# A hybrid decoder trunk on one core: x's scales inside the transposing matmul, convolution buffers of their own, and the weights' low parts split over two engines

## The chip, the cores and the metric

The kernel runs on one core of one Trainium2 chip. The metric is the device time of one execution in microseconds. Three runs of the kernel before are given, with a median of 2076.28 us, and one of its executions was profiled.

A core has a matrix engine (TensorE, PE in the profile; its weight loads are PEld), a vector engine (VectorE, DVE), an activation engine (ScalarE, ACT), a general engine (GpSimd, POOL) and a queue that issues most transfers (SyncE, SP). Each engine works through its own list of instructions in order and waits where an operand is not ready.

## The reference

One decoder layer over 2048 tokens of 1024 channels. The normalised input goes through one projection, whose columns feed three groups of heads; their gated outputs are joined, projected back and added to the input.

```python
u = rms_norm(h, norm_g[l])
proj = jnp.einsum('bsd,de->bse', u, w_in[l])
(q, k, v, z_att, f_raw, z_ssd, xbc, dt_raw, x_lru, z_lru) = jnp.split(proj, split_points, axis=-1)
log_f = jax.nn.log_sigmoid(f_raw + forget_b[l])
y_att = fox_attention(q, k, v, log_f, q_norm_g[l], k_norm_g[l]) * jax.nn.silu(z_att)
y_ssd = ssd_mixer(xbc, dt_raw, z_ssd, ...)      # causal convolution, silu, chunked scan, gated norm
y_lru = rglru_mixer(x_lru, ...) * jax.nn.silu(z_lru)   # causal convolution, gates, associative scan
mix = jnp.concatenate([y_att, y_ssd, y_lru], axis=-1)
h = h + jnp.einsum('bse,ed->bsd', mix, w_out[l])
```

`rms_norm` divides each token's row by the root of its mean square and multiplies by a gain for each channel. Everything is float32.

## The kernel before, in words

PE multiplies in a rounded float32 (`F32R`). A float32 operand is split into a high part (rounded by a cast) and a low part (the remainder, by a subtraction), and each product is made of three matmuls: high times high, and the two mixed ones. So u exists as `uh`, `ul` and a weight tile as `wh`, `wl`.

The stages, in the order in which PE meets them (times of the profiled execution):

- **x** (9 to 67 us). x is loaded in 16 tiles `xt` of 128 tokens by 1024 channels, four tiles to a block of tokens `tb`. For each tile ACT squares and sums (L255, with an accumulator read), DVE and ACT make `rs` = 1/root (L127 to L131), DVE scales the tile by it (L264, in block 0), and PE transposes it in 128x128 pieces (L279, the float32 identity as one operand) into a PSUM tile `pu`, one for each of 8 slices k of 128 channels. ACT writes `uh` from `pu` (L282) and DVE `ul` (L283).
- **Convolution groups** (16 to 322 us). Six groups of 256 columns (`pxx`, `proj_ch`, L331 to L333), each 4 token blocks by 2 halves, 24 matmuls of 128x512 a piece. Each piece goes through `conv`: ACT copies it out of PSUM into `rtx` (L376), ACT starts the sum `accx` (L381), DVE adds three more taps (L384), ACT takes tanh (L409, into a buffer `thx`), DVE multiplies; the result goes to DRAM, by PE transposes for the first groups and straight from `accx` for the last (`ct_d`). Group 0 runs between the transposes of x.
- **pvz** (322 to 376 us): 280 columns for all 16 token tiles (`proj_tok`, L305 to L307). DVE reads its last columns for `dt` (L367).
- **LRU** (377 to 596 us), four groups m of 128+128 columns: projections `pll` and `pzl`, each convolution and split again into `xhl`, `xll`, gates `pga`, `pgx` (L561 to L563), then on DVE reciprocals (L569), a scan over 1024 tokens (L585) and on POOL and ACT the gate path.
- **zs** (582 to 774 us): four groups of 256 columns, two token tiles into one PSUM tile (`proj_tok2`, L318 to L320). Then the same function for q, k and v, z of attention, with units of the SSD scan between them (to 1275 us).
- **Attention and output projection**, to the end.

What sets the order: the kernel text states the work, and a scheduler with a cost simulation (`schedule_with_timeline_sim=True`) fixes each engine's list when the kernel is built. A change of buffers or of the engine of one instruction can so move others.

Weights: `weights()` (L178) loads 8 tiles of 128 rows for each group into raw buffers `wr` (pool `wrp`, 4 buffers), casts each on ACT (L192) and subtracts on the engine `eng` (L193): DVE by default, POOL for the LRU groups and the first two zs groups. The pool `wp` holds `NSL` = 9 tiles `wh` and as many `wl`, one more than a group has.

Buffers: the convolution's pool `cvp` (tags `acc`, `thx`, `stx`, 2 buffers each) is opened after the pools of the x stage are closed, and `accx` has two buffers.

Of the kernel before, what the change touches and what calls it, by code (L numbers as in the profile page):

```python
# [18 lines left out]
P = 128  # L19
# [7 lines left out]
NEG = -1.0e30  # L27
NSL = 9
NQ = 4
# [18 lines left out]
def hybrid_block(ctx, tc, x, norm_g, w_in, q_norm_g, k_norm_g, forget_b, ssd_conv_w, ssd_conv_b,  # L48
# [128 lines left out]

    def weights(cols, rawp=wrp, eng=V):  # L178

        n = sum(w for _, w in cols)  # L180
        i = gcount[0]
        gcount[0] += 1
        wh, wl = [], []
        for k in range(KD):
            raw = rawp.tile([P, n], F32, name=f"wr{i}_{k}", tag="wr")
            h = wp.tile([P, n], F32R, name=f"wh{i}_{k}", tag="wh")
            l = wp.tile([P, n], F32R, name=f"wl{i}_{k}", tag="wl")
            o = 0
# [3 lines left out]
            A.copy(h, raw)  # L192
            eng.tensor_tensor(l, raw, h.bitcast(F32), op=ALU.subtract)  # L193
            wh.append(h)
            wl.append(l)
        return wh, wl, n

    rtx = ExitStack()
    rtp = rtx.enter_context(tpool(name="rtp", bufs=2, side="right"))
    with tpool(name="p0", bufs=2) as p0, tpool(name="p01", bufs=1) as p01, \  # L200
            tpool(name="px", bufs=XB) as px:
# [43 lines left out]
        def c1(name, i=0):  # L245
            j = CV[name] + i
            return cv[:, j:j + 1]

        def norm_x(tb):
            ss = p0.tile([P, 4], F32, name=f"ss{tb}", tag="ss")  # L250
            rs = p0.tile([P, 4], F32, name=f"rs{tb}", tag="rs")
            for i in range(4):
                t = tb * 4 + i
                sq = p01.tile([P, D], BF16, name=f"sq{t}", tag="sq")
                A.activation(sq, xts[t], AF.Square, accum_out=ss[:, i:i + 1])  # L255
                if tb == 0:
                    rsqrt1(p0, rs[:, i:i + 1], ss[:, i:i + 1], 1.0 / D, f"r0{t}")
            if tb > 0:
                V.tensor_scalar(ss, ss, 1.0 / D, EPS, op0=ALU.mult, op1=ALU.add)
                rsqrt(p0, rs, ss, 4, f"r0{tb}")  # L260
            for i in range(4):
                xt = xts[tb * 4 + i]
                if tb == 0:
                    V.tensor_scalar(xt, xt, rs[:, i:i + 1], -1.0, op0=ALU.mult, op1=ALU.mult)  # L264
                elif i < NDV:
# [6 lines left out]
        for tb in range(4):  # L272
            if tb + AHEAD < 4:
                norm_x(tb + AHEAD)
            for k in range(KD):
                pt, tag = ((psY, "Y"), (pst, "pt"))[(tb * KD + k) % 5 % 2]
                pt = pt.tile([P, 512], F32, name=f"pu{tb}_{k}", tag=tag)
                for i in range(4):
                    T.transpose(pt[:, i * P:(i + 1) * P],  # L279
                                xts[tb * 4 + i][:, k * P:(k + 1) * P], ident)  # L280
                g = ngc[:, k:k + 1]
# [27 lines left out]

    def proj_tok2(w, t2, name, space=None):  # L310
        wh, wl, n = w
        pp, tag = space or (psj, "pj")
        ps = pp.tile([P, 2, 256], F32, name=name, tag=tag)
        for i in range(2):
            t = t2 * 2 + i
            h, l, sl = uh[t // 4], ul[t // 4], slice(t % 4 * P, t % 4 * P + P)
            for k in range(KD):
                T.matmul(ps[:, i, :], h[k][:, sl], wh[k], start=(k == 0), stop=False)  # L318
                T.matmul(ps[:, i, :], h[k][:, sl], wl[k], start=False, stop=False)  # L319
                ins = T.matmul(ps[:, i, :], l[k][:, sl], wh[k], start=False, stop=(k == KD - 1))  # L320
        anchor[0] = ins
# [51 lines left out]

    def conv(pool, ps, prev, wname, bname, m, nm, ntile, acc, tag="", rtp=None):
        rt = (rtp or pool).tile([P, 515], F32, name=f"rt{nm}", tag="rt" + tag)
        A.copy(rt[:, 3:515], ps)  # L376
# [12 lines left out]
    g0 = g0x.enter_context(tpool(name="g0", bufs=2))  # L389
    with tpool(name="cvp", bufs=2) as pool, tpool(name="cl", bufs=1) as cl:  # L390
        for gq in range(6):
# [9 lines left out]
            for tb in range(4):  # L401
                for mm in range(2):
                    m = gq * 2 + mm
                    nm = f"x{m}_{tb}"
                    ps = proj_ch(w, mm, tb, f"px{nm}")
                    acc = pool.tile([P, 512], F32, name=f"acc{nm}", tag="acc")
                    prev[mm] = conv(pool, ps, prev[mm], "cw", "cb", m, nm, 12, acc, str(mm), rtp)
                    th = pool.tile([P, 512], F32, name=f"thx{nm}", tag="thx")
                    A.activation(th, acc, AF.Tanh)  # L409
# [4 lines left out]
                    if m < 10:  # L414
                        pt = pst.tile([P, 4, P], F32, name=f"ptx{nm}", tag="pt")
                        for i in range(4):
                            T.transpose(pt[:, i, :], acc[:, i * P:(i + 1) * P], ident)
                        st = pool.tile([P, 4, P], F32, name=f"st{nm}", tag="stx")
                        A.copy(st, pt)
# [670 lines left out]
```

## Time and profile before

| quantity | value |
|---|---|
| runs | 2074.33, 2076.28, 2081.79 us (median 2076.28) |
| profiled execution | 2074.41 us, its span 2072.7 us |
| PE busy | 2002.1 us, 97% of the span |
| PEld busy | 1759.0 us, 85% |
| DVE busy | 1246.1 us, 60% |
| ACT busy | 975.9 us, 47% |
| POOL busy | 568.9 us, 27% |
| bytes moved | 265.18 MB, mean 128 GB/s |

The time of an execution and its span differ by 1.7 us, which lie outside the profile. In rows of the timeline the columns are the start, the busy time, engine, line, operation, output and inputs, tile shape, count, and in brackets the idle time before and what ended it. In windows each engine has its busy time and its number of instructions, and `PEclk` is the granted clock of PE as a share of full speed. Durations of matmuls overlap, so that the time that one costs in a stream is the distance between two starts.

### The profile page before, as it was taken

Reading aid. Unit: us, or ns where it says so; the run is one execution under the profiler, and the core shown is the slowest. Engines: PE = TensorE matmul, PEld = TensorE weight load, DVE = VectorE, ACT = ScalarE, POOL = GpSimd, SP = SyncE. Lnnn points to the kernel's source line nnn. Section 1 sums busy time; section 2 is a strip of 40 time slices with the busy share of each in tenths; the row PEclk is TensorE's granted clock in tenths of the full one; section 3 lists DMA queues with packets and bytes.
Section 4 is the critical chain, followed back from the end, with each engine's and each line's share of the span. In section 5 each row is a group of like instructions: output and inputs, shape, how many; then the busy total and the mean of one; then the engine's idle time right before and its main releaser. Section 6 shows DMA issues by size and latency. Waiting matters only on the chain. (4 is left out here: it accounts for less than half of the span.)

```text
span 2072.7 us, 36031 instructions
## 1 busy us (share of the span) xinstructions
PE 2002.1 (97%) x12485; PEld 1759.0 (85%) x12485; DVE 1246.1 (60%) x2656; ACT 975.9 (47%) x2053; POOL 568.9 (27%) x814
## 2 busy tenths in 40 slices
PE   7999999999999999999998999999998999999999
PEld 6788888887789998887887998888887888888887
DVE  6655455388875226776566345667767777775333
ACT  7444443366652124554444234566666666664110
POOL 0000001355531004454553001243332333323110
PEclk9999999999999999999999999999999999999999
DMA  5122233111123225666655726575475375443443
GB/s 197 41 70 63 62 113 102 44 42 43 42 62 99 69 76 148 197 196 191 195 173 161 214 85 218 159 200 160 131 192 163 115 193 151 133 129 91 136 142 117
DMA packets 287317, 265.18 MB, mean 128 GB/s; under 512 B 59780, under 2 KB 227232, under 8 KB 285088
## 3 DMA queue, kind: packets, MB, share of 16 engines
q1 hardware_dynamic: 286976, 262.85, 43.3%
q8 instruction: 99, 1.62, 0.3%
q14 instruction: 82, 0.67, 0.1%
q0 software_dynamic: 160, 0.03, 0.1%
HBM read 168.22 MB, written 94.57 MB: 127 GB/s over the span
## 5 line engine op out<-in xcount | busy, mean ns | idle before, releaser
L918 DVE TENSOR_TENSOR pl<-T,ph 128x512 fp32r<-128x512 f32 (+2 forms) x352 | 191.1, 565 | 70.8 <-ACT ph L917 69.5
L980 PE MATMUL po<-woh,mh 128*128 128x512 f32 x512 | 213.0, 416 | 8.9 <-DVE xr L988 4.7
L917 ACT CAST ph<-T 128x512 fp32r<-128x512 f32 (+2 forms) x352 | 161.9, 490 | 122.6 <-PE T L910 84.9
L981 PE MATMUL po<-wol,mh 128*128 128x512 f32 x512 | 201.5, 394 | 0.0
L982 PE MATMUL po<-woh,ml 128*128 128x512 f32 x512 | 200.5, 397 | 0.0
L910 PE MATMUL T<-ident,L 128*128 128x128 f32 x1088 | 172.6, 276 | 2.4 <-ACT L L860 1.5
L860 ACT ACTIVATE L<-L,mx 128x1920 f32<-128x1920 f32 (+15 forms) x128 | 154.5, 1208 | 39.7 <-DVE mx L857 35.2
L384 DVE SCALAR_TENSOR_TENSOR accx<-rtx,cv,accx 128x512 f32<-128x512 f32 x144 | 104.5, 752 | 90.9 <-ACT accx L381 76.0
L331 PE MATMUL pxx<-uh,wh 128*128 128x512 f32 x384 | 153.0, 401 | 4.8 <-ACT rtx L376 3.3
L319 PE MATMUL pqk<-wl,uh 128*128 128x256 f32 x512 | 153.6, 301 | 2.6 <-DVE wl L193 2.6
L896 PE MATMUL O<-ph,vv 128*128 128x256 f32 x576 | 153.8, 288 | 2.0 <-ACT ph L917 1.9
L332 PE MATMUL pxx<-ul,wh 128*128 128x512 f32 x384 | 153.9, 402 | 0.0
L897 PE MATMUL O<-pl,vv 128*128 128x256 f32 x576 | 152.2, 289 | 1.0 <-DVE pl L918 0.7
L333 PE MATMUL pxx<-uh,wl 128*128 128x512 f32 x384 | 152.8, 399 | 0.0
L318 PE MATMUL pqk<-wh,uh 128*128 128x256 f32 x512 | 147.1, 292 | 3.1 <-ACT wh L192 3.1
L320 PE MATMUL pqk<-wh,ul 128*128 128x256 f32 x512 | 149.5, 294 | 0.0
L319 PE MATMUL pzs<-wl,uh 128*128 128x256 f32 x512 | 144.8, 284 | 3.2 <-POOL wl L193 3.1
L320 PE MATMUL pzs<-wh,ul 128*128 128x256 f32 x512 | 144.5, 283 | 0.0
L318 PE MATMUL pzs<-wh,uh 128*128 128x256 f32 x512 | 143.2, 283 | 0.0
L648 ACT ACTIVATE ab<-ab,nacs 128x128 f32<-128x128 f32 x256 | 82.6, 391 | 125.9 <-POOL ab L644 125.7
L849 POOL TENSOR_SCALAR_AFFINE_SELECT cm<-cb 128x384 f32<-128x384 f32 (+3 forms) x128 | 58.9, 463 | 297.8 <-DVE mx L857 145.3
L910 PEld LDWEIGHTS T<-ident,L 128*128 128x128 f32 x1088 | 127.4, 141 | 13.5 <-ACT L L860 5.4
(315 smaller groups left out, 5600.9 us busy)
## 6 DMA issues: line engine op xcount, KB each, us to landing
ab<-acs_d SPq DMA_DIRECT2D x64, 256.0 KB
pt_d<-xr SPq DMA_DIRECT2D x64, 256.0 KB
wr<-in_w_in_dram SPq DMA_DIRECT2D x192, 64.0 KB
wr<-in_w_in_dram SPq DMA_DIRECT2D x80, 128.0 KB
xt<-in_x_dram SPq DMA_DIRECT2D x16, 512.0 KB
xs_d<-stx SPq DMA_DIRECT2D x32, 256.0 KB
v_d<-vs SPq DMA_DIRECT2D x32, 256.0 KB
zs_d<-zs SPq DMA_DIRECT2D x32, 256.0 KB
```

The lines of the kernel that those rows point to most:

```text
L318: T.matmul(ps[:, i, :], h[k][:, sl], wh[k], start=(k == 0), stop=False)
L319: T.matmul(ps[:, i, :], h[k][:, sl], wl[k], start=False, stop=False)
L320: ins = T.matmul(ps[:, i, :], l[k][:, sl], wh[k], start=False, stop=(k == KD - 1))
L332: T.matmul(ps, wh[k][:, ms], ul[tb][k], start=False, stop=False)
L860: A.activation(lt[:, 0:n], lt[:, 0:n], AF.Exp, bias=mx, scale=-1.0, accum_out=sm[:, i:i + 1])
L896: T.matmul(po[:, ca], vv[:, kt, :], ph[:, jj, ca], start=(kt == 0), stop=False)
L910: ins = T.transpose(pt[:, jj, i * P:(i + 1) * P], L[i][:, kt * P:(kt + 1) * P], ident)
L917: A.copy(ph[:, ja, ca], pt[:, ja, ca])
L918: V.tensor_tensor(pl[:, ja, ca], pt[:, ja, ca], ph[:, ja, ca].bitcast(F32), op=ALU.subtract)
L980: T.matmul(ps, mh[:, j, :], h, start=(j == 0), stop=False)
L981: T.matmul(ps, mh[:, j, :], l, start=False, stop=False)
L982: T.matmul(ps, ml[:, j, :], h, start=False, stop=(j == 3))
```

## The change

1. **x, block 0.** The tiles are no longer scaled (L264 falls away). Instead DVE writes `dg`, the identity times `-rs`, 128x128 for each of the four tiles, and PE multiplies the 128x128 piece of x with `dg` in an ordinary float32 matmul in place of the transpose (32 of them). Tiles 1 and 3 are squared on DVE, 0 and 2 on ACT as before. The table for the square root is loaded ahead of all of it.
2. **Convolution buffers.** `cvp` (now for `stx` and `dg`) and `cv3` (`acc`, 3 buffers) are opened ahead of the pools of x and share no memory with them. The tanh goes into the first 512 columns of the `rtx` tile, so that there is no `thx`.
3. **`NSL`** is 8 and no longer 9.
4. **`proj_tok2`** runs k outside and the two token tiles inside: a weight tile serves six matmuls in a row.
5. **Low parts.** In the LRU groups and the first two zs groups, POOL subtracts for even k and DVE for odd k.

The diff, cut to its core:

```diff
-NSL = 9
+NSL = 8
-    def weights(cols, rawp=wrp, eng=V):
+    def weights(cols, rawp=wrp, eng=(V,)):
-            eng.tensor_tensor(l, raw, h.bitcast(F32), op=ALU.subtract)
+            eng[k % len(eng)].tensor_tensor(l, raw, h.bitcast(F32), op=ALU.subtract)
...
+    cvp = rtx.enter_context(tpool(name="cvp", bufs=2, side="right"))
+    cv3 = rtx.enter_context(tpool(name="cv3", bufs=3, side="right"))
...
+        dg = cvp.tile([P, 4, P], F32, name="dg", tag="stx")
+        A.activation(p01.tile([P, 1], F32, name="tab"), eps, AF.Sqrt)
...
+                if tb == 0 and i % 2:
+                    sq = cv3.tile([P, D], BF16, name=f"sq{t}", tag="acc")
+                    V.tensor_tensor_reduce(sq, xts[t], xts[t], 1.0, 0.0, ALU.mult, ALU.add,
+                                           ss[:, i:i + 1])
+                else:
...
                 if tb == 0:
                     rsqrt1(p0, rs[:, i:i + 1], ss[:, i:i + 1], 1.0 / D, f"r0{t}")
+                    V.tensor_scalar(dg[:, i, :], ident, rs[:, i:i + 1], -1.0, op0=ALU.mult,
+                                    op1=ALU.mult)
...
-                    V.tensor_scalar(xt, xt, rs[:, i:i + 1], -1.0, op0=ALU.mult, op1=ALU.mult)
+                    continue
...
-                    T.transpose(pt[:, i * P:(i + 1) * P],
-                                xts[tb * 4 + i][:, k * P:(k + 1) * P], ident)
+                    xk = xts[tb * 4 + i][:, k * P:(k + 1) * P]
+                    if tb == 0:
+                        T.matmul(pt[:, i * P:(i + 1) * P], xk, dg[:, i, :], start=True, stop=True)
+                    else:
+                        T.transpose(pt[:, i * P:(i + 1) * P], xk, ident)
...
-        for i in range(2):
-            t = t2 * 2 + i
-            h, l, sl = uh[t // 4], ul[t // 4], slice(t % 4 * P, t % 4 * P + P)
-            for k in range(KD):
-                T.matmul(ps[:, i, :], h[k][:, sl], wh[k], start=(k == 0), stop=False)
+        for k in range(KD):
+            for i in range(2):
+                t = t2 * 2 + i
+                h, l, sl = uh[t // 4], ul[t // 4], slice(t % 4 * P, t % 4 * P + P)
+                last = k == KD - 1
+                T.matmul(ps[:, i, :], h[k][:, sl], wh[k], start=(k == 0 and i == 0), stop=False,
+                         skip_group_check=True)
...
-    with tpool(name="cvp", bufs=2) as pool, tpool(name="cl", bufs=1) as cl:
+    with tpool(name="cl", bufs=1) as cl:
...
-                    acc = pool.tile([P, 512], F32, name=f"acc{nm}", tag="acc")
-                    th = pool.tile([P, 512], F32, name=f"thx{nm}", tag="thx")
+                    acc = cv3.tile([P, 512], F32, name=f"acc{nm}", tag="acc")
+                    th = prev[mm][:, 0:512]
...
-            w = weights([(C_XL + m * P, P), (C_ZL + m * P, P)], eng=G)
+            w = weights([(C_XL + m * P, P), (C_ZL + m * P, P)], eng=(G, V))
...
-            w = weights([(C_ZS + gq * 256, 256)], eng=G if gq < 2 else V)
+            w = weights([(C_ZS + gq * 256, 256)], eng=(G, V) if gq < 2 else (V,))
```

How it moves instructions, at the three places of which the prediction speaks. In the lists, the first number of a name is the token block or tile, or the slice k of a weight tile, and the last is a running number that differs between the two kernels.

At the head, DVE's list of the kernel before, from the low parts of the first weight tiles to the scaling of the fourth tile of x:

```order
L193 TENSOR_TENSOR wl_0_235<-wr_0_233,wh_0_234 128x256
L193 TENSOR_TENSOR wl_1_241<-wr_1_239,wh_1_240 128x256
L129 RECIPROCAL rs_323<-r_t 128x1
L193 TENSOR_TENSOR wl_2_247<-wr_2_245,wh_2_246 128x256
L130 SCALAR_TENSOR_TENSOR r_t<-rs_323,r_h 128x1
L193 TENSOR_TENSOR wl_3_253<-wr_3_251,wh_3_252 128x256
L131 SCALAR_TENSOR_TENSOR rs_323<-r_t,rs_323 128x1
L264 TENSOR_SCALAR xt_231<-xt_231,rs_323 128x1024
```

The same place of the changed kernel, from the second low part to the fourth tile's `dg`; the square of the fourth tile, an operation named ISA, stands four rows further up, with the first low part behind it:

```order
L193 TENSOR_TENSOR wl_1_247<-wr_1_245,wh_1_246 128x256
L219 COPY ngc<-pr 128x8
L128 TENSOR_SCALAR r_h<-ss_331 128x1
L130 SCALAR_TENSOR_TENSOR r_t<-rs_332,r_h 128x1
L193 TENSOR_TENSOR wl_2_253<-wr_2_251,wh_2_252 128x256
L129 RECIPROCAL rs_332<-r_t 128x1
L193 TENSOR_TENSOR wl_3_259<-wr_3_257,wh_3_258 128x256
L131 SCALAR_TENSOR_TENSOR rs_332<-r_t,rs_332 128x1
L130 SCALAR_TENSOR_TENSOR r_t<-rs_332,r_h 128x1
L268 TENSOR_SCALAR dg<-ident,rs_332 128x128
L131 SCALAR_TENSOR_TENSOR rs_332<-r_t,rs_332 128x1
L268 TENSOR_SCALAR dg<-ident,rs_332 128x128
```

The third tile's `dg` and the fourth's have moved behind the square on DVE and behind all four low parts; before, the third tile was scaled ahead of the low parts and only the fourth behind them.

At the end of the convolution groups, ACT's list of the kernel before, from a copy of the last block to the last tanh (pvz's own copies L356 and L362 stand between):

```order
L409 ACTIVATE thxx_2_2951<-accx_2_2943 128x512
L356 ACTIVATE vs_0_3110<-pvz_0_3112 128x2x64
L356 ACTIVATE vs_0_3110<-pvz_1_3137 128x2x64
L356 ACTIVATE vs_1_3178<-pvz_2_3180 128x2x64
L381 ACTIVATE accx_3_2980<-rtx_3_2981,cv 128x512
L362 ACTIVATE th_0_0_3164<-pvz_0_3112 128x128
L362 ACTIVATE th_0_1_3171<-pvz_1_3137 128x128
L381 ACTIVATE accx_3_3017<-rtx_3_3018,cv 128x512
L362 ACTIVATE th_1_0_3232<-pvz_2_3180 128x128
L409 ACTIVATE thxx_3_2988<-accx_3_2980 128x512
L409 ACTIVATE thxx_3_3025<-accx_3_3017 128x512
```

The same place of the changed kernel:

```order
L397 COPY rtx_3_2941<-pxx_3_2915 128x512
L192 CAST wh_0_2998<-wr_0_2997 128x280
L402 ACTIVATE accx_3_2940<-rtx_3_2941,cv 128x512
L192 CAST wh_1_3007<-wr_1_3006 128x280
L192 CAST wh_2_3016<-wr_2_3015 128x280
L192 CAST wh_3_3025<-wr_3_3024 128x280
L192 CAST wh_4_3034<-wr_4_3033 128x280
L431 ACTIVATE rtx_3_2941<-accx_3_2940 128x512
L397 COPY rtx_3_2977<-pxx_3_2951 128x512
L192 CAST wh_5_3043<-wr_5_3042 128x280
L402 ACTIVATE accx_3_2976<-rtx_3_2977,cv 128x512
L192 CAST wh_6_3052<-wr_6_3051 128x280
```

Before, the last four sums L381 and tanhs stand behind the weight casts and behind copies of pvz's own results; now each piece is copied, summed and put through tanh within a few rows, with the casts of pvz's weights between.

At the boundary between two LRU groups, DVE's list of the kernel before, around the first scan of a group, beside which the next group's weights are made:

```order
L584 TENSOR_TENSOR XC_0_4606<-XC_0_4606,MM_0_4711 128x1024
L585 SCALAR_TENSOR_TENSOR MM_0_4711<-RA_0_4710,XC_0_4606 128x1024
L588 COPY hc_0_4821<-MM_0_4711 128x1
L589 SCALAR_TENSOR_TENSOR ZZ_0_4679<-MM_0_4711,ZZ_0_4679 128x1024
L568 TENSOR_SCALAR RA_1_4922<-RA_1_4922 128x512
L569 RECIPROCAL RA_1_4922<-RA_1_4922 128x512
L568 TENSOR_SCALAR RA_1_4922<-RA_1_4922 128x512
```

The same place of the changed kernel:

```order
L607 SCALAR_TENSOR_TENSOR MM_0_4670<-RA_0_4669,XC_0_4565 128x1024
L193 TENSOR_TENSOR wl_1_4937<-wr_1_4935,wh_1_4936 128x256
L610 COPY hc_0_4780<-MM_0_4670 128x1
L611 SCALAR_TENSOR_TENSOR ZZ_0_4638<-MM_0_4670,ZZ_0_4638 128x1024
L193 TENSOR_TENSOR wl_3_4951<-wr_3_4949,wh_3_4950 128x256
L193 TENSOR_TENSOR wl_5_4965<-wr_5_4963,wh_5_4964 128x256
L590 TENSOR_SCALAR RA_1_4881<-RA_1_4881 128x512
L591 RECIPROCAL RA_1_4881<-RA_1_4881 128x512
L193 TENSOR_TENSOR wl_7_4979<-wr_7_4977,wh_7_4978 128x256
L590 TENSOR_SCALAR RA_1_4881<-RA_1_4881 128x512
L591 RECIPROCAL RA_1_4881<-RA_1_4881 128x512
```

The four odd low parts of the next group now stand in DVE's list, the first directly behind the scan, two behind the product L611 and the last behind a reciprocal.

More of the change, by code (lines that the diff above doesn't have):

```diff
@@ L313, in proj_tok2 @@
         ps = pp.tile([P, 2, 256], F32, name=name, tag=tag)
-        for i in range(2):
-            t = t2 * 2 + i
-            h, l, sl = uh[t // 4], ul[t // 4], slice(t % 4 * P, t % 4 * P + P)
-            for k in range(KD):
-                T.matmul(ps[:, i, :], h[k][:, sl], wh[k], start=(k == 0), stop=False)
-                T.matmul(ps[:, i, :], h[k][:, sl], wl[k], start=False, stop=False)
-                ins = T.matmul(ps[:, i, :], l[k][:, sl], wh[k], start=False, stop=(k == KD - 1))
+        for k in range(KD):
[5 more added lines that the diff above has]
+                         skip_group_check=True)
+                T.matmul(ps[:, i, :], h[k][:, sl], wl[k], start=False, stop=False,
+                         skip_group_check=True)
+                ins = T.matmul(ps[:, i, :], l[k][:, sl], wh[k], start=False, stop=last,
+                               skip_group_check=True)
         anchor[0] = ins
@@ L371, in group_vz, with conv @@
             dma(za_d[p][rr, :].rearrange("(i p) c -> p i c", p=P), zt)
-    def conv(pool, ps, prev, wname, bname, m, nm, ntile, acc, tag="", rtp=None):
-        rt = (rtp or pool).tile([P, 515], F32, name=f"rt{nm}", tag="rt" + tag)
+    def conv(pool, ps, prev, wname, bname, m, nm, ntile, acc, tag=""):
+        rt = pool.tile([P, 515], F32, name=f"rt{nm}", tag="rt" + tag)
         A.copy(rt[:, 3:515], ps)
@@ L405, in hybrid_block @@
                     ps = proj_ch(w, mm, tb, f"px{nm}")
[L406 to L408 removed]
+                    acc = cv3.tile([P, 512], F32, name=f"acc{nm}", tag="acc")
+                    prev[mm] = conv(rtp, ps, prev[mm], "cw", "cb", m, nm, 12, acc, str(mm))
+                    th = prev[mm][:, 0:512]
                     A.activation(th, acc, AF.Tanh)
@@ L417, in hybrid_block @@
                             T.transpose(pt[:, i, :], acc[:, i * P:(i + 1) * P], ident)
-                        st = pool.tile([P, 4, P], F32, name=f"st{nm}", tag="stx")
+                        st = cvp.tile([P, 4, P], F32, name=f"st{nm}", tag="stx")
                         A.copy(st, pt)
```

6 lines of the change are left out of this document (3 added, 3 removed).

## The prediction

> **What bounds the kernel now.** I read the page first, then PE's waits up to 1260 us, then windows by stage, then the timeline around each long wait.
>
> ```profile
> PE 2002.1 (97%) x12485; PEld 1759.0 (85%) x12485; DVE 1246.1 (60%) x2656; ACT 975.9 (47%) x2053; POOL 568.9 (27%) x814
> ...
> PE pvz L305 <- DVE dt L367: 3.6, 1, 3.6
> PE pxx L331 <- ACT rtx L376: 3.3, 1, 3.3
> PE pll L333 <- POOL wl L193: 3.2, 4, 1.5
> PE pqk L318 <- ACT wh L192: 3.1, 2, 2.5
> PE pzs L319 <- POOL wl L193: 3.1, 3, 1.8
> PE pqk L319 <- DVE wl L193: 2.6, 2, 1.6
> ...
> PE pxx L331 <- ACT uh L282: 1.5, 2, 1.2
> ```
>
> PE bounds the whole: 97% busy, and no other engine over 60%. The matmuls of the projections stay as many as they were, so the change can only take out PE's waits (the lines give their sum, number and longest), what a wait does to PE's clock, or add work to PE. The rows that the change addresses sum to 20.4 us, under 1% of 2074. A wait also costs beyond its idle time, which windows behind the waits show:
>
> ```profile
> 0.00:67.00 67.00, 55.16 (x280) 44.89 (x281) 40.58 (x114) 47.89 (x85) 2.76 (x13) 1.00 0.45 152
> ...
> 74.50:78.80 4.30, 4.29 (x12) 3.41 (x13) 3.40 (x16) 2.08 (x5) 0.25 (x1) 0.61 0.22 58
> 334.80:338.30 3.50, 3.50 (x15) 3.50 (x16) 3.30 (x11) 1.61 (x3) 0.00 (x0) 0.51 0.15 45
> 587.40:594.30 6.90, 6.65 (x26) 5.74 (x26) 4.25 (x3) 3.94 (x8) 5.08 (x7) 0.51 0.56 169
> 857.00:864.00 7.00, 6.99 (x28) 5.75 (x28) 6.17 (x20) 3.65 (x11) 2.69 (x3) 0.51 0.69 197
> ```
>
> After these waits the granted clock (third number from the end) is 0.51 to 0.61, over 3.5 to 7 us. At 0.51 a window does half the work, so the last three lose 1.7, 3.4 and 3.4 us, and the first 4.30 x 0.39 = 1.7 us. A wait that ends early takes its slow stretch with it.
>
> **The change part by part.** The sum is made against the profiled execution, 2074.41 us, span 2072.7.
>
> *Head.* Rows of x's first block, with the nearest prices of the new operations:
>
> ```profile
> 5.91 1.28 ACT L127 ACT_TABLE_LOAD   x1
> ...
> 9.87 3.33 PE L279 MATMUL pu<-ident,xt 128*128 128x128 f32 x13
> 14.36 1.33 PE L279 MATMUL pu<-ident,xt 128*128 128x128 f32 x5 [1.15 <-DVE xt L264]
> 16.02 1.22 PE L331 MATMUL pxx<-uh,wh 128*128 128x512 f32 x2 [0.34 <-ACT uh L282]
> ...
> 10.29 1.04 ACT L255 ACTIVATE sq<-xt 128x1024 bf16<-128x1024 f32 x1
> ...
> 13.03 0.42 DVE L193 TENSOR_TENSOR wl<-wr,wh 128x256 fp32r<-128x256 f32 x1
> 13.55 0.75 DVE L264 TENSOR_SCALAR xt<-xt,rs 128x1024 f32<-128x1024 f32 x1
> ...
> 644.48 0.38 PE L479 MATMUL pc<-lf,tri 128*128 128x128 f32 x2
> 644.70 0.39 PE L483 MATMUL pc<-lf,ones 128*128 128x128 f32 x2
> 644.84 0.36 PE L319 MATMUL pzs<-wl,uh 128*128 128x256 f32 x1
> ...
> 64.41 0.60 PE L279 MATMUL pu<-ident,xt 128*128 128x128 f32 x4
> 64.76 0.48 PE L332 MATMUL pxx<-ul,wh 128*128 128x512 f32 x1
> ...
> L857 DVE CUSTOM_DVE_ANT_0 L<-S,cb x96: 677/688/694, 1273.8 to 1871.9; 128x512 f32<-128x512 f32 x96
> ```
>
> Removed: four scalings of 0.75 us on DVE, and the table load at 5.91 from the chain of the first tile. The first tile's transposes start earlier, but the fourth tile ends the stage. Its square moves from ACT (10.29) to DVE; the nearest row of a DVE pass with an accumulator is L857, 0.69 for 512 columns, so about 1.3 for 1024. Tile 4 is the last to land; with ACT's 10.29 as its earliest start, it ends at 11.6 to 12.0 (estimate). Behind it DVE has four low parts at 0.43 (1.7 us), some nine small steps at about 0.16 and two `dg` at about 0.2, so the last `dg` comes at about 15.4, where the last scaled tile came at 14.30 (13.55 + 0.75). In front of the first `pxx` wait ten matmuls with `dg` (those of tiles 3 and 4, since both `dg` come late), before only five transposes.
>
> The price of a plain float32 matmul of 128 columns: L479 has two records for its one matmul, 0.22 us from start to start of the next line, and L483 0.14 to 0.22. A transpose in a warm stream takes (64.76 - 64.41)/4 = 0.09, one at the head 1.33/5 = 0.27. So ten at the head take 2.2 us at full clock and 4.3 at half (twice). `pxx` then starts near 17.3 or 19.4, against 16.02: +1.3 to +3.4. The other 12 (k = 5 to 7) cost 0.13 more each, +1.6. Against it, the wait of 1.2 us for `uh` (PE's waits, above) ends where the transfers of x set it and swallows as much. Sum +1.7 to +3.8; I take +2.4, between them but nearer the full clock, since ten matmuls back to back leave few slow ones behind them. Ends: 0 (clock up early) and +5 (ACT's interleaved convolution also lags).
>
> The rule of the Trainium skill that speaks loudest against this edit is in "FP8 and Floating Point Precision" (TensorE Precision Notes): a true float32 product takes four passes through the array. By it a matmul would take 4 x 0.09 = 0.36 us or more, and the head another 4 us; the trace's 0.22 at L479 disagrees for this size, so I keep the row.
>
> *Convolution, start and end.*
>
> ```profile
> 67.90 1.51 ACT L381 ACTIVATE accx<-rtx,cv 128x512 f32<-128x512 f32 x2
> 73.35 0.63 ACT L409 ACTIVATE thxx<-accx 128x512 f32<-128x512 f32 x1 [2.42 <-DVE accx L384]
> ...
> 74.51 0.50 PE L331 MATMUL pxx<-uh,wh 128*128 128x512 f32 x1 [3.28 <-ACT rtx L376]
> ...
> 325.23 0.81 ACT L381 ACTIVATE accx<-rtx,cv 128x512 f32<-128x512 f32 x1 [1.53 <-DMA ct_d<-accx]
> ...
> 334.81 0.54 PE L305 MATMUL pvz<-wh,uh 128*128 128x280 f32 x1 [3.57 <-DVE dt L367]
> ...
> L384 DVE SCALAR_TENSOR_TENSOR accx<-rtx,cv,accx 128x512 f32<-128x512 f32 x144 | 104.5, 752 | 90.9 <-ACT accx L381 76.0
> ```
>
> The first sum L381 runs at 67.90, right after x's last transposes, since its buffers share memory with x's. PSUM fills, and PE stops for 3.28 us before 74.51 and restarts at a low clock: 3.3 + 1.7 = 5.0. With memory of their own the sums run inside the x stage, as the new list of ACT shows. That stage must then hold six more pieces: ACT 47.89 + 6 x (0.8 for the sum, 0.63 for the tanh, about as much for the copy) = 60 of 67 us, DVE 40.58 + 6 x 4 passes x 0.75 = 59 of 67. It fits narrowly, so I charge 0.8: -4.2 (ends -5.0 and 0).
> At the end, sums wait for the transfer of the last result out of the same buffer (325.23, others alike), convolutions run late into pvz, DVE reaches `dt` late and PE waits 3.57, then 1.7 for the clock: 5.2. With a third `acc` and no pile-up I take -4.7, since one tail remains ahead of `dt` (ends -5.3 and 0).
>
> *Low parts and slots in the LRU groups.*
>
> ```profile
> 526.75 3.27 DVE L585 TENSOR_TENSOR_SCAN MM<-RA,XC 128x1024 f32<-128x1024 f32 x1
> ...
> 528.30 6.00 POOL L193 TENSOR_TENSOR wl<-wr,wh 128x256 fp32r<-128x256 f32 x5 [0.43 <-ACT wh L192]
> 538.74 0.74 POOL L193 TENSOR_TENSOR wl<-wr,wh 128x256 fp32r<-128x256 f32 x1
> ...
> 530.60 0.50 PE L333 MATMUL pll<-uh,wl 128*128 128x512 f32 x1 [1.53 <-POOL wl L193]
> ...
> 533.03 0.40 ACT L192 CAST wh<-wr 128x256 fp32r<-128x256 f32 x1 [3.89 <-DMA wr<-in_w_in_dram]
> 535.01 3.35 DVE L569 RECIPROCAL RA<-RA 128x512 f32<-128x512 f32 x1
> ```
>
> POOL alone needs 0.74 for a low part; five beside the scan took 6.00, so 2.3 us are lost to it, and PE waits (530.60). Halving POOL's share helps the later ones. But the odd parts stand behind the scan in DVE's list: `wl_1` comes at 530.02 + 0.43 = 530.5, where POOL had it near 529.5, and the raw buffer that it frees is the one for which the cast at 533.03 waits, so that cast moves up to 1 us later. With `NSL` 8, `wl_0` too is made at the boundary. DVE idles until its reciprocal at 535.01, so `wl_3` and `wl_5` cost its chain nothing; `wl_7` behind it is ready when its raw tile is. I take +0.5 at each of four boundaries, +2. Ends: -4 (pll's 3.2 and some clock go) and +6 (1.5 each).
>
> *k outside in `proj_tok2`, 8 slots.*
>
> ```profile
> 854.03 1.28 ACT L648 ACTIVATE ab<-ab,nacs 128x128 f32<-128x128 f32 x4 [5.79 <-POOL ab L644]
> ...
> 855.65 0.51 PE L318 MATMUL pqk<-wh,uh 128*128 128x256 f32 x2 [2.54 <-ACT wh L192]
> ```
>
> A weight tile's last reader comes earlier: with k outside, the first tile of a group is free 42 of 48 matmuls before its end, before 21, so casts can run 21 matmuls sooner, and a group's start needs a new tile only every six matmuls. Waits here: pzs 3.1, pqk 3.1 and 2.6, so 8.8, and slow windows worth 3.4 + 3.4 (587.4 and 857). Of these 15.6 the largest (855.65) has its cast in ACT's list behind exponentials that wait for POOL, which freeing slots doesn't touch; also the scheduler already interleaved two token tiles at a group's start. I take -6 (ends 0 and -14).
>
> Sum: +2.4 - 4.2 - 4.7 + 2 - 6 = -10.5, so 2063.9. The median lies 1.9 above the profiled execution: 2065.8, forecast 2066.
>
> **The rivals.**
> *Group starts keep their waits* (-6 becomes 0, all else alike): 2072. For it: the scheduler's own interleaving, and the blocked cast at 854. Against: earlier free slots.
> *The stalls go more fully*: head 0, LRU -3, `proj_tok2` -10: 2066 - 2.4 - 5 - 4 = 2054.6, say 2055. For it: slow stretches come off in lumps of 1.7 to 3.4 us. The Trainium skill, "TensorE: Matmul & The Clock Gate" (Part 4), says that transposes do not count as work that raises the clock, so that real matmuls with `dg` would raise it sooner and the head would come out near 0; the head's 0.27 a transpose, after 5 us of them, agrees that they had not raised it.
> *DVE's low parts become the new wait* (slower side): place, the six groups that POOL and DVE share; if `wl_7` or an earlier odd part is needed while a reciprocal (3.35) runs, PE waits 3.35 and then loses 1.7 for the clock, 5 a group, 30 in all: 2066 - 2 + 30 = 2094. It decides from 4 us a group on (2066 - 2 + 24 = 2088, over +0.5%). Against it: DVE idles before the reciprocal, and its raw tiles come late anyway.
>
> **How the numbers follow.** Half a per cent, 10.4 us, is about what a measurement of this kernel tells from no change; the bounds are 2065.9 and 2086.7. My forecast has 0.45 (own range 2060 to 2072, half under the bound: 0.24 faster, 0.21 same). Group starts that keep their waits 0.22 (same). Fuller gains 0.24 (faster). The low parts as a wait 0.09 (0.07 slower, 0.02 same). Together 0.48, 0.45, 0.07. The range 2053 to 2077 takes in all but the last and the outer tails of the second and third.
>
> **What would show it.** First `pxx` near 17 to 19 us; no idle over 1 us at 70 to 75 and at 331 to 335, and no 0.5 clock behind them; sums L402 inside the first 67 us; waits of pll for POOL or DVE `wl` of 3 to 6 us in sum; waits of pzs and pqk for weights halved. Attention must keep its length, since PE's list from there on is the same; if it doesn't, a cause that I have not costed is at work. I'd be wrong if x's stage were stretched by the convolution, or if the freed waits came back as waits for transfers of weights.

## The result, and the profile after

The changed kernel took 2068.26 us (median of 9 runs, 2060.26 to 2073.0), the kernel before 2078.41 in the same series (2072.84 to 2081.79). The ratio is 0.9946, with a 95% interval of 0.9929 to 0.9963: 0.5% faster. The forecast was 2066, with a range of 2053 to 2077, on the edge between faster and no change. Its sum held; several of its terms did not. The kernel before was slower in this series than in the three runs that the forecast was made from (2078.41 against 2076.28).

The times at which PE reaches the marks of the two profiled executions (starts of the first or last matmul of a name, from the trace) show where. One execution of each kernel was profiled, and nine of the changed kernel alone lie 13 us apart, so a difference of a few microseconds at one mark is an indication, not a proof:

| mark | before | after | difference | its stretch alone | forecast |
|---|---|---|---|---|---|
| first `pxx` | 16.0 | 16.7 | +0.7 | | |
| last transpose of x | 67.0 | 73.9 | +6.9 | | |
| end of the convolution groups | 321.5 | 322.1 | +0.5 | +0.5 | +2.4 - 4.2 |
| end of pvz | 376.3 | 372.9 | -3.5 | -4.0 | -4.7 |
| last `pgx` of LRU | 596.5 | 591.8 | -4.6 | -1.1 | +2 |
| end of zs | 774.4 | 770.3 | -4.1 | +0.5 | -6, with the next |
| first S of attention | 1257.3 | 1248.5 | -8.8 | -4.6 | |
| last output | 2067.7 | 2060.7 | -7.0 | +1.7 | 0 |

PE's waits of the changed kernel up to 1260 us (who waits for whom: sum, times, longest):

```profile
PE py L675 <- DVE ab L671: 7.5, 7, 2.6
PE pll L354 <- POOL wl L193: 4.5, 4, 1.8
PE pxx L352 <- ACT uh L297: 3.4, 2, 1.9
...
PE pzs L338 <- POOL wl L193: 2.8, 3, 2.2
...
PE py L675 <- ACT wh L192: 2.2, 1, 2.2
...
PE pvz L320 <- DVE dt L388: 1.1, 1, 1.1
```

The wait for `rtx` at 74.5 us (3.3) is gone, and of the 3.6 for `dt` 1.1 is left. The waits of q, k and v for weights (3.1 + 2.6 before) have shrunk to one of 2.2. Waits for `uh` and for POOL's low parts in LRU have grown: 1.5 to 3.4, and 3.2 to 4.5. So has that of `py` for `ab`, which was 1.0 us before and is now the largest of these: the waits of q, k and v's stretch have changed their place more than their sum (PE idles 19.4 us there, 22.1 before).

The head, in PE's timeline and then DVE's, of the changed kernel (start, busy time, idle before in brackets):

```profile
8.22 2.08 PE L293 MATMUL pu<-dg,xt 128*128 128x128 f32 x8 [8.22 <-DVE dg L268]
...
14.29 2.50 PE L293 MATMUL pu<-dg,xt 128*128 128x128 f32 x20 [0.60 <-DVE dg L268]
16.67 0.74 PE L352 MATMUL pxx<-uh,wh 128*128 128x512 f32 x2
...
18.68 0.39 PE L354 MATMUL pxx<-uh,wl 128*128 128x512 f32 x1
18.91 0.40 PE L352 MATMUL pxx<-uh,wh 128*128 128x512 f32 x1
```

```profile
10.87 1.22 DVE L261 CUSTOM_DVE_ANT_0 sq<-xt 128x1024 bf16<-128x1024 f32 x1
...
14.34 0.29 DVE L268 TENSOR_SCALAR dg<-ident,rs 128x128 f32<-128x128 f32 x1
```

Each matmul has two records. At 8.22 four take 2.08 us, 0.52 each; at 14.29 ten take 2.50, 0.25 each, so the clock is up by then. At 18.68 the distance from `pxx` to `pxx` is 0.23. Before, matmuls of that size were 0.43 apart until 20.5:

```profile
19.18 0.63 PE L332 MATMUL pxx<-ul,wh 128*128 128x512 f32 x1
19.61 0.63 PE L333 MATMUL pxx<-uh,wl 128*128 128x512 f32 x1
20.03 0.63 PE L331 MATMUL pxx<-uh,wh 128*128 128x512 f32 x1
```

What x's second block now waits for, in ACT's list and on PE:

```profile
32.37 1.05 ACT L265 ACTIVATE sq<-xt 128x1024 bf16<-128x1024 f32 x1
33.33 0.19 ACT L265 ACTIVATION_READ_ACCUMULATOR sq<-xt 128x1 f32 x1
33.42 0.56 ACT L397 COPY rtx<-pxx 128x512 f32<-128x512 f32 x1
33.89 0.81 ACT L402 ACTIVATE accx<-rtx,cv 128x512 f32<-128x512 f32 x1
34.60 0.67 ACT L297 ACTIVATE uh<-pu,ngc 128x512 fp32r<-128x512 f32 x1
```

```profile
35.33 0.72 PE L352 MATMUL pxx<-uh,wh 128*128 128x512 f32 x2 [1.95 <-ACT uh L297]
```

The first `uh` of the block stands behind a square of the block after, a copy and a sum of the convolution; in the kernel before, it followed the copy directly.

### The profile page after: what moved, and what is told of

Read it like the earlier page. It is cut to its first block, busy times and chain, and to the rows that moved or that the text cites. A ratio compares the mean times of both kernels' runs of the same rounds, so it can differ in the third digit from the quotient of the medians.

```text
span 2065.2 us, 36048 instructions
## 1 busy us (share of the span) xinstructions
PE 2000.1 (97%) x12517; PEld 1756.8 (85%) x12517; DVE 1268.8 (61%) x2684; ACT 978.6 (47%) x2049; POOL 542.1 (26%) x790
## 5 line engine op out<-in xcount | busy, mean ns | idle before, releaser
L1002 PE MATMUL po<-woh,mh 128*128 128x512 f32 x512 | 213.0, 416 | 10.2 <-DVE xr L1010 5.3
L338 PE MATMUL pqk<-wl,uh 128*128 128x256 f32 x512 | 145.9, 285 | 0.0
```

Of the source, the lines that this page charges most:

```text
L1002: T.matmul(ps, mh[:, j, :], h, start=(j == 0), stop=False)
```

## The experiments

Twelve kernels, in three series with the kernel before beside each. The common base is the kernel before with the convolution's buffers (they need the memory of the ninth weight slot, so it has 8). The first table has that base with the head, the loop and the split of the low parts in all eight combinations; all three together are the changed kernel, whose row is from the first measurement. Ratios are to the kernel before of the same series.

| kernel | head | loop | low parts | ratio, 95% | last transpose of x | LRU, us | end of zs to S, us |
|---|---|---|---|---|---|---|---|
| buffers | old | old | POOL | 0.9990, 0.9974 to 1.0005 | 76.2 | 219.0 | 482.6 |
| + split | old | old | split | 0.9990, 0.9976 to 1.0003 | 76.1 | 219.9 | 485.3 |
| + loop | old | new | POOL | 0.9948, 0.9927 to 0.9968 | 71.9 | 216.8 | 481.8 |
| + head | new | old | POOL | 0.9927, 0.9905 to 0.9950 | 72.4 | 218.6 | 472.5 |
| old head | old | new | split | 0.9959, 0.9941 to 0.9978 | 73.6 | 218.7 | 478.5 |
| POOL only | new | new | POOL | 0.9946, 0.9926 to 0.9967 | 71.5 | 216.5 | 478.5 |
| old loop | new | old | split | 0.9950, 0.9933 to 0.9967 | 75.2 | 221.0 | 473.7 |
| changed kernel | new | new | split | 0.9946, 0.9929 to 0.9963 | 73.9 | 219.0 | 478.3 |

The last three columns are distances of marks in one profiled execution each (LRU from the end of pvz to the last `pgx`, the last column from the end of zs to the first S).

**Buffers alone.** The edit is the second part of the change, and `NSL = 8`:

```diff
+    cvp = rtx.enter_context(tpool(name="cvp", bufs=2, side="right"))
+    cv3 = rtx.enter_context(tpool(name="cv3", bufs=3, side="right"))
+                    th = prev[mm][:, 0:512]
```

> The kernel before with the convolution's own buffers (third acc, tanh into the rtx tile) and NSL 8, which pays for their memory; head, loop and low parts as before. Theory A (the gain at 74.5 us is given back inside the x stage, because the convolution's sums now stand between x's work on ACT and DVE; the head itself costs nothing): the convolution groups end at 322 +- 1 us as in the changed kernel, pvz is 4 us shorter, the whole 3 to 5 us under before. Theory B (the new head cost the 5 us that the buffers had gained): the groups end near 317, pvz is 4 us shorter, the whole 8 to 10 us under before.

Measured 0.9990: no clear gain. The stall at 74.5 is gone and pvz is 4 us shorter (50.8), but x's last transposes come 9 us later and the groups end at 324.3, 2.8 later than before. PE's waits and ACT's list of this kernel:

```profile
PE pxx L333 <- ACT uh L284: 5.9, 3, 4.2
```

```profile
33.84 1.06 ACT L257 ACTIVATE sq<-xt 128x1024 bf16<-128x1024 f32 x1
34.80 0.19 ACT L257 ACTIVATION_READ_ACCUMULATOR sq<-xt 128x1 f32 x1
34.89 0.57 ACT L378 COPY rtx<-pxx 128x512 f32<-128x512 f32 x1
35.35 0.82 ACT L383 ACTIVATE accx<-rtx,cv 128x512 f32<-128x512 f32 x1
36.07 1.84 ACT L284 ACTIVATE uh<-pu,ngc 128x512 fp32r<-128x512 f32 x3
```

So the gain of the buffers at the start is given back inside the x stage, without any new head: theory A is right on the place, B falls. Its numbers are missed (324.3 and not 322, 2 us under the kernel before and not 3 to 5).

How much is given back varies. The kernels with the split, the loop, and loop and split added to the buffers have the same lists up to the last transpose of x, row by row, and their groups end at 324.3, 320.1 and 321.8; the waits of `pxx` for `uh` are 6.0, 3.2 and 4.8 us. Part of it is the clock. Behind its wait of 4.2 us the buffers kernel runs at half clock for 6.8 us, which costs about 3.4 (an estimate: half of it); in the same window the kernel with the loop has the full clock. Windows of both, the buffers kernel first (the third number from the end is the clock):

```profile
35.90:42.70 6.80, 5.90 (x18) 4.60 (x19) 6.67 (x15) 4.74 (x9) 0.00 (x0) 0.50 0.00 0
```

```profile
35.90:42.70 6.80, 6.80 (x37) 5.64 (x35) 6.80 (x14) 5.39 (x8) 0.00 (x0) 1.00 0.30 95
```

Differences of up to 4 us at the end of the groups are therefore not proof of an edit.

**The old head.** The changed kernel without `dg`, DVE squares and early table.

> The changed kernel with the old head: x's first block scaled on DVE, transposes, all squares on ACT, no early table load. Theory A: groups end within 1.5 us of the changed kernel's 322.1, the first pxx 0.7 us earlier at 16.0 but PE at half clock to about 21 us; the whole within 2 us of the changed kernel. Theory B: groups end near 317.5, the whole 4 to 5 us under the changed kernel.

Measured 0.9959, groups' end at 321.8 beside 322.1, as theory A had it; B falls. With the new loop the head is worth nothing that can be seen, with POOL alone either (0.9946 with it, 0.9948 without).

**Low parts.** The changed kernel with `eng=(G,)`, and the buffers kernel with the split alone:

> The changed kernel with all low parts of the LRU and first zs groups on POOL again. Theory C (the split is worth nothing, as the first tiles wait for the scan either way): LRU to the last pgx within 1.5 us of the changed kernel's 219.0 us, whole the same. Theory D (8 slots alone would cost some 3 us in LRU and the split buys it back): LRU 222 us or more and the whole 3 us over the changed kernel. My prediction's term (+2 for the split) would show as LRU 217 us or less.

> The buffers kernel with the low parts split over POOL and DVE alone added. Theory C (worth nothing): LRU 218 to 220 us, ratio 0.998 to 1.000. Theory D: LRU 217 or less, ratio 0.997 or less. My prediction's term (+2 us): LRU 221, ratio 1.000.

Neither ratio moves (0.9946 beside 0.9946, 0.9990 beside 0.9990). In the two other pairs of the table it is higher with the split (0.9959 for 0.9948, 0.9950 for 0.9927), with intervals that overlap. The stretch of LRU is longer with the split in all four pairs, by 0.9, 1.9, 2.4 and 2.5 us. With POOL alone it is 216.5, as the prediction's term had it; the split added to the buffers gives 219.9, as theory C had it; D falls. The waits move too. PE's waits in LRU, first of the kernel with POOL alone, then of the one with the split added to the buffers:

```profile
PE pll L354 <- POOL wl L193: 1.9, 2, 1.2
```

```profile
PE pll L344 <- POOL wl L193: 4.9, 4, 1.8
```

The split more than doubles the wait that it was put against (in the changed kernel it is 4.5, in the buffers kernel without the split 1.8). DVE's and POOL's timelines of the changed kernel at a boundary, and POOL's of the kernel with POOL alone at the same one, show why:

```profile
524.98 2.28 DVE L607 TENSOR_TENSOR_SCAN MM<-RA,XC 128x1024 f32<-128x1024 f32 x1
527.18 0.88 DVE L193 TENSOR_TENSOR wl<-wr,wh 128x256 fp32r<-128x256 f32 x1
527.99 0.14 DVE L610 COPY hc<-MM 128x1 f32<-128x1 f32 x1
528.05 2.23 DVE L611 SCALAR_TENSOR_TENSOR ZZ<-MM,ZZ 128x1024 f32<-128x1024 f32 x1
530.21 0.95 DVE L193 TENSOR_TENSOR wl<-wr,wh 128x256 fp32r<-128x256 f32 x1
```

```profile
525.30 2.48 POOL L193 TENSOR_TENSOR wl<-wr,wh 128x256 fp32r<-128x256 f32 x1 [10.14 <-ACT wh L192]
```

```profile
520.54 2.29 POOL L554 TENSOR_TENSOR xll<-XC,xhl 128x512 fp32r<-128x512 f32 x1 [8.62 <-ACT xhl L553]
522.79 3.78 POOL L193 TENSOR_TENSOR wl<-wr,wh 128x256 fp32r<-128x256 f32 x4
```

With the split, POOL's first low part stands beside the scan and takes 2.48; the one on DVE behind the scan takes 0.88 to 0.95 beside POOL. By themselves they take 0.74 and 0.42. A low part beside a scan is no new thing: in the kernel before, the first at each of the four boundaries took 2.24 to 2.26. With the buffers and POOL alone another instruction (`xll`) stands beside the scan at three boundaries of four, and the low parts come behind it, the first at 1.70 beside DVE's product and the others at 0.73. So the split brings back an order that the buffers had done away with. LRU takes 218.7 to 221.0 us in four kernels with the split in the table, 216.5 to 219.0 in four without.

**The loop.** The changed kernel with the old loop, and the buffers kernel with the new loop alone:

> The changed kernel with the old loop of proj_tok2 (token tile outside, k inside), still 8 slots. Theory E (k outside frees slots earlier and lets the weights of the next group be made in time): the stretch from the first pqk to the first S is 4 us or more longer than the changed kernel's 478.0 us and waits for weights (pqk, pvz, pzs) come back to 8 us or more; whole 4 to 8 us over the changed kernel. Theory F (the gain in that stretch is another interleaving of the list only): within 1.5 us of the changed kernel, weight waits under 4 us.

> The buffers kernel with the new loop of proj_tok2 alone added. Theory E (earlier free weight slots): pqk, pvz and pzs wait for weights 3 us less, stretch from the first pqk to the first S near 478.5, ratio to before 0.9965 to 0.9975. Theory F (nothing; the length of that stretch varies by 4 us and more between executions of one and the same list): ratio as the buffers kernel, 0.998 to 1.000.

Measured 0.9950 and 0.9948. Theory E falls: with the old loop the stretch of q, k and v is 473.7 us, 4.6 shorter than the changed kernel's, not 4 longer (F, which allowed 1.5 either way, is missed too). Nor do weight waits come back with the old loop: in that stretch the buffers kernel waits 2.4 and 0.6 us for `wh`, where the kernel before waited 7.6 for weights in all. The changed kernel with the old loop waits 2.1. So most of them are gone in the buffers kernel already, with one slot fewer and another list, and without the loop. The loop alone on the buffers does give a lower ratio (0.9948 beside 0.9990), lower than either theory allowed. But its profile is shorter in the x stage and LRU, where the loop plays no part, and by only 0.8 us in the stretch where it runs. In this pair of profiles the clock is behind much of it: the buffers kernel ran at half clock for 6.8 us in the x stage and for 6.8 at 585.5, together about 3.4 + 3.4 us (an estimate), and the kernel with the loop not at all between 21 and 888 us. Why the timed runs differ is open. Together with the new head it gives nothing more (0.9946 beside 0.9927, the intervals overlap).

**The head alone, and its parts.** The buffers kernel with the new head; with the early table alone; with table and `dg`; with table and DVE squares:

> The buffers kernel (first experiment) with the new head alone added. Theory A (the head is worth nothing in the end, as the transfers of x's second block set when PE goes on): groups end within 1.5 us of the buffers kernel's, whole within 0.15% of it (ratio to before 0.997 to 1.000). Theory G (head worth some -0.2%, from a clock that is up earlier): ratio 0.9965 to 0.9975.

> The buffers kernel with the square root's table loaded first: one small activation more, and every other list the same to the last row. Theory H (the 10 us between the stretches of q, k, v with SSD units, 483 and 473 us under the same lists, hang on small shifts that the head makes, not on work saved in it): the stretch can go either way; if it is 473 here too, such a shift is enough, and the whole is 0.994 of before. Theory I (the head's own work is what matters: the dg matmuls or the squares): stretch 482 to 485 us, ratio 0.998 to 1.000, head itself 1 us earlier at most.

> The buffers kernel with the early table and the matmuls with dg, all squares still on ACT. Theory J (dg carries the head's gain: the clock is up before the first pxx and the scalings of 0.75 us are gone): ratio 0.993 to 0.995, PE at full clock by 17 us. Theory K (the squares on DVE carry it): ratio 0.998 to 1.000.

> The buffers kernel with the early table and tiles 1 and 3 of block 0 squared on DVE, but the old scaling and transposes. Theory J: ratio 0.998 to 1.000, PE at half clock to about 20 us. Theory K: ratio 0.993 to 0.995.

| kernel | ratio, 95% | last transpose of x | end of groups | end of zs to S, us |
|---|---|---|---|---|
| + head | 0.9927, 0.9905 to 0.9950 | 72.4 | 320.6 | 472.5 |
| table | 0.9978, 0.9964 to 0.9993 | 75.3 | 323.5 | 478.6 |
| table, dg | 0.9927, 0.9909 to 0.9946 | 72.4 | 320.5 | 473.4 |
| table, squares | 0.9956, 0.9940 to 0.9973 | 69.8 | 318.0 | 480.3 |

With the old loop `dg` is worth half a per cent: its interval and that of the table alone, on the same chip, do not meet. Theory J holds for `dg`, but for the squares alone neither J nor K does: 0.9956 lies between them, and PE is at full clock by 18.6, not 20. The whole head is worth more than theory A or G had allowed. With the early table alone the stretch, 478.6, lies between I's 482 to 485 and the 473 that would have shown H, and the ratio is just under I's range. With `dg`, x and the groups end 3 us sooner, which is no more than kernels with the same lists differ there, and PE is at full speed by 17.9 at the latest. PE's timeline of the kernel with table and dg:

```profile
15.90 0.72 PE L348 MATMUL pxx<-uh,wh 128*128 128x512 f32 x2 [0.61 <-ACT uh L297]
...
17.92 0.40 PE L350 MATMUL pxx<-uh,wl 128*128 128x512 f32 x1
18.15 0.39 PE L348 MATMUL pxx<-uh,wh 128*128 128x512 f32 x1
```

The spans of the kernels with the table and with table and `dg` are 11.3 us apart, 3.0 of them by the end of the groups. Of the rest, 5.2 us lie hundreds of microseconds later, in a stretch where the lists of all five engines are the same to the row, and 4.0 in attention, under one list too, where a single wait of PE for `xr` near the end (7.4 us in one, 3.7 in the other) is nearly all of it; LRU is 0.9 longer. Windows of the stretch before attention, of the kernel with the table and of that with table and dg (span, then PE busy; the last three numbers are granted clock, share and rate of transfers):

```profile
770.60:1249.20 478.60, 457.23 (x3497) 421.24 (x3496) 289.25 (x547) 209.73 (x571) 180.11 (x181) 0.99 0.61 177
```

```profile
768.50:1241.90 473.40, 453.75 (x3498) 419.50 (x3497) 289.06 (x548) 210.09 (x572) 178.19 (x181) 0.99 0.62 179
```

The same matmuls keep PE busy for 457 or for 454 us (457 in the buffers kernel, 453 with the whole head), and it idles the rest longer or shorter. The busy time differs with the clock, which a mean of 0.99 hides. With the table alone there are four spells at half clock in this stretch, with table and dg two:

```profile
839.30:842.70 3.40, 2.88 (x13) 2.89 (x14) 3.37 (x5) 1.20 (x4) 3.32 (x4) 0.51 0.78 221
931.50:934.90 3.40, 3.40 (x9) 1.82 (x7) 2.29 (x4) 0.00 (x0) 1.97 (x2) 0.50 0.30 98
975.90:979.30 3.40, 3.40 (x12) 2.37 (x11) 2.16 (x6) 2.18 (x7) 1.04 (x1) 0.50 0.73 238
1102.20:1105.60 3.40, 2.98 (x14) 2.98 (x15) 3.37 (x5) 1.14 (x5) 3.32 (x4) 0.50 0.64 150
```

```profile
865.30:868.70 3.40, 3.40 (x18) 3.40 (x17) 3.25 (x6) 2.37 (x8) 0.04 (x1) 0.50 0.93 246
1097.40:1100.80 3.40, 3.40 (x18) 3.40 (x17) 2.48 (x3) 1.45 (x5) 2.41 (x2) 0.50 0.64 205
```

At half of its length each, a spell costs 1.7 us (an estimate), so 3.4 of the 5.2 us are clock. In attention it is the other way round, and over both whole profiles the spells cost the same, about 17 us. Nor are they the timed half per cent: by the mean spans of the timed runs (2072.1 and 2061.2 us) and their mean clocks (0.9900 and 0.9910), 2 of the 11 us are clock, an estimate.

POOL's wait for the loads of `ab` differs too, here of the buffers kernel and of the one with the head:

```profile
POOL ab L646 <- DMA ab<-acs_d: 65.8, 37, 5.5
```

```profile
POOL ab L662 <- DMA ab<-acs_d: 42.0, 29, 5.3
```

But this doesn't part the groups: it is 55.0 with table and dg, and 49.7 with the squares alone.

Theory H holds in so far as the stretch varies under one list: 478.6 to 485.3 in the four kernels with the old loop and without `dg`, where the spells cost 6.8 to 8.5 us. The four with the old loop and `dg` lie at 472.5, 473.4, 473.7 and 477.2, all under that, with 1.7 to 5.1 us for the spells. All four have lower timed ratios than the others, though the highest, 0.9950, is not parted from the lowest of the others, 0.9956. Whether `dg` shortens this stretch, or these single executions fell so, is not shown, and neither is what would carry it besides the clock: it is not the order of instructions, and not the start of the stretch either (766 to 773 us in both groups).

**Squares of every block on two engines.** First on the changed kernel, then on the buffers kernel with the new head, old loop and POOL:

```diff
-                if tb == 0 and i % 2:
+                if i % 2:
```

> The changed kernel with tiles 1 and 3 of every block, not of block 0 alone, squared on DVE, whose list there has idle stretches of 2 to 5 us. Theory A (in the x stage uh comes late, as ACT has squares, scaling and now the convolution's sums ahead of it): the waits of pxx for uh at 33 and 52 us fall from 3.4 us to under 1.5, x's last transposes come before 71 us instead of 73.9, the groups end at 318 to 320, whole 2 to 4 us under the changed kernel. Rival (the transfers of x, whose 8 buffers are freed only by the transposes, set the stage): last transposes still at 73 or later, whole the same.

> The buffers kernel with the new head and the squares of tiles 1 and 3 of every block on DVE; old loop, low parts on POOL. If the two gains seen apart add up (head alone 0.9927; squares in every block brought x's last transposes 3 us forward): ratio 0.991 to 0.992, groups end near 318, about 2060 us, under both kernels. If the rest eats it (the sums come later into the convolution groups): 0.9925 to 0.994.

On the changed kernel x's last transposes come at 70.7 us and the groups end at 318.9, as theory A had it. That is 3 us under the changed kernel, and 0.8 to 4.5 under the four kernels that have its lists of the x stage (319.7 to 323.4). The ratio is 0.9936 (0.9911 to 0.9960), which its interval does not part from 0.9946. On the other kernel the wait for `uh` all but goes. PE's waits, and ACT's list, of it:

```profile
PE pxx L348 <- ACT uh L297: 0.3, 1, 0.3
```

```profile
30.32 1.04 ACT L265 ACTIVATE sq<-xt 128x1024 bf16<-128x1024 f32 x1
31.27 0.19 ACT L265 ACTIVATION_READ_ACCUMULATOR sq<-xt 128x1 f32 x1
31.36 1.05 ACT L393 COPY rtx<-pxx 128x512 f32<-128x512 f32 x2
32.30 3.75 ACT L297 ACTIVATE uh<-pu,ngc 128x512 fp32r<-128x512 f32 x6
```

It took 2060.96 us, ratio 0.9919 (0.9901 to 0.9936), with the groups' end at 318.2, as the first expectation had it: the lowest ratio of all, clearly under the kernel before, and 0.3% under the changed kernel's ratio with intervals that just overlap. It is not parted from the head alone (0.9927).

## Why the prediction was right or wrong

**The sum** was 10.5 us, measured were 10.2 by the medians and 7.0 to 7.5 in the two profiles. That is better than its terms deserve, and so partly luck: in the profiles the convolution groups came 2.3 us worse than forecast, pvz 0.7, zs to S 1.9 and attention 1.7, and LRU 3.1 better.

**Head, +2.4: wrong; it costs nothing, and gains with the old loop.** The steps on DVE were right within a microsecond (the square 1.22 against 1.3; the last `dg` done at 14.6, not 15.4, as small steps overlap), and so was the price of a matmul, 0.25 us against 0.22. (That 0.09 us, a transpose's price, is also that of one of four passes was my assumption, so 0.25 says nothing against four passes.) What failed is the step that left the clock to an end of the range. Ordinary matmuls had raised it by 14.3 us, whereas transposes from 9.1 to 15.7 had not raised it until 20.5. The rule of the Trainium skill that I had put beside a rival ("TensorE: Matmul & The Clock Gate", Part 4: transposes don't count as work that raises the clock) agrees with both traces. It agrees with the others too: in all seven executions with transposes PE was still at half speed at the first `pxx`, and at full speed only from 18.3 to 21.2 us on; with `dg` six of seven had it by 14.3. The seventh, the changed kernel with the old loop, had the same lists there and stayed at half until 17.7 (sixteen matmuls at 0.50 each):

```profile
10.04 7.97 PE L293 MATMUL pu<-dg,xt 128*128 128x128 f32 x32
```

So `dg` didn't always bring the clock up early. With the old loop and POOL alone it is worth -0.5%; with the new loop the whole head is worth nothing.

**Convolution, start, -4.2: wrong.** The stall went as told, for the reason told. The failed step is "it fits narrowly, so I charge 0.8": I set sums of busy time against the length of the stage. What counted was what stood ahead of `uh` on ACT at the moment PE had nothing else, and in four of the five kernels with the buffers, all squares on ACT and the old scaling, a spell at half clock followed a wait there. In these five the groups ended between 1.4 us earlier and 2.8 later than in the kernel before (320.1, 321.8, 323.5, and 324.3 twice), not 4.2 earlier. The rival of a stretched x stage, named at the end of the prediction, is the one that came; with two squares of each block on DVE the wait for `uh` falls to 0.3 us or less.

**pvz, -4.7: right**, at -4.0 in every kernel with the buffers.

**Low parts, +2: right in sign and size, not in mechanism.** The split lengthens LRU by 0.9 to 2.5 us, and the wait for POOL's parts is 4.5 to 5.8 us with it (changed kernel and four others) and 1.8 or 1.9 with the buffers and without it, about +3. I had charged the odd parts on DVE, which stand behind the scan; what PE waits for is POOL's parts, the first of which the split puts beside the scan. The changed kernel's LRU was nevertheless 1.1 us shorter than before, since the base with the buffers, 8 slots and POOL alone is shorter (216.5 to 219.0, its wait 1.8 and no longer 3.2); I had counted the 8 slots as a cost. Contention of DVE's own parts (0.88 to 0.95 for 0.42) I had not costed.

**`proj_tok2`, -6: near in place and size by luck, wrong in cause.** zs was 0.5 longer and the stretch behind it 4.6 shorter, but single executions with the old loop vary between 472 and 485 there under one list, and the loop was not seen to shorten it: the old loop beside the rest of the change gives 473.7.

**Attention, 0:** the stretch from the first S on is 1.7 us longer in the changed kernel's profile, under the same list of PE; the other profiles vary more than that (810 to 819 us). One spell at half clock more would be as much.

## What to carry to other kernels

Before giving a stage more work because its engines have room on average, look at which instruction of that engine releases the bound engine, and what will stand ahead of it in its list. When several edits come together, add them to a common base one by one and in pairs: here one of five worked against its aim (the split), one added nothing beside the head (the loop), and the version with the lowest ratio lacks both. A difference of a few microseconds in one stretch of a single profile is no proof of a cause, where kernels with the same lists differ by 4 at the start and by 13 later; look first whether spells at half clock account for it.

## What the hardware showed that I had not expected

DVE and POOL slow each other: a low part of 0.74 us took 2.48 on POOL beside a scan on DVE, and one of 0.42 took 0.88 to 0.95 on DVE beside POOL. Float32 matmuls of 128 columns with `dg` had PE at full clock 4 to 6 us after the first in six executions (0.52 us each at 8.2, 0.25 at 14.3) and after 10 us in the seventh, while transposes of the same shape did not raise it before the first `pxx` in any of seven. And instruction lists that are the same to the row took 472 to 485 us over one stretch in eight executions, with PE busy for 452 to 459 of it. Between 1.7 and 8.5 us of that are spells at half clock, 3.4 or 6.8 us long each, an estimate at half of their length; what makes up the rest, and whether an edit far ahead of it moved it, stays open.
